# Expert weights in 16 KB runs laid out for them, four turned banks, a scatter in two groups, and another order of steps before and after the experts

## The chip, the cores and the metric

The kernel runs on one core of a Trainium2 chip. The core has TensorE (PE, matrix products into the 8 banks of PSUM), VectorE (DVE), ScalarE (ACT), GpSimd (POOL) and SyncE (SP), which issues most of the transfers from HBM to SBUF; 16 DMA engines carry them. The metric is the device time of one execution in microseconds (us), the median of the runs shown.

## The reference

Two layers follow each other on x of 512 tokens by 1024 channels, all float32.

```
def first_block(...):
    h = rmsnorm(x, norm1_g);  p = h @ w_in            # 1024 -> 1536
    c = centred_depthwise_conv(lru_x, conv_w, conv_b)
    h_f, h_b = rglru(c, ..., reverse=False), rglru(c, ..., reverse=True)
    y_lru = gelu(lru_gate) * (h_f + h_b);  y_four = fourier_mix(four_in)
    x = x + concat(y_lru, y_four) @ w_out
    x = x + expert_choice_moe(rmsnorm(x, norm2_g), w_router, w_gate, w_up, w_down)
    return rmsnorm(x, normf_g)

def expert_choice_moe(h, ...):                        # 16 experts, 64 tokens each
    gate, idx = top_k(softmax(h @ w_router).T, 64)    # each expert picks its tokens
    g, u = xin @ w_gate[e], xin @ w_up[e]             # xin = h[idx]; 1024 -> 2048
    eo = (silu(g) * u) @ w_down[e]                    # 2048 -> 1024
    out[idx] += gate * eo

def second_block(...):
    q, k, v, z_a, u, z_s, g_a, g_s = split(rms_norm(x, gain) @ w_in_2)
    y_a = (band_attention(q, k, v, rel_bias) * silu(z_a)) @ w_attn_out
    y_s = (glu(gelu(s5_ssm(u, ...))) * silu(z_s)) @ w_ssm_out
    return rms_norm(x + (sigmoid(g_a) * y_a + sigmoid(g_s) * y_s) @ w_out_2, final_gain)
```

The expert weights are 16 x 3 x 1024 x 2048 numbers, 402.65 MB, and each is read once.

## The kernel before, in words

The engines run what the source writes in the order in which it writes it; waits come from the data and from buffers that come free.

**Stage 1** (line numbers of the kernel before): `in_proj` units (weights in [128, 1024] pieces of 512 KB, loaded and split into a high and a low part by `Stream`, lines 126 to 159), convolution, gates, recurrence, Fourier part, `w_out`, router. A product of two float32 operands is three matmuls (`mm3`, lines 120 to 123): high by high, high by low, low by high. A "unit" is 24 such matmuls with 512 columns. The sums of squares of x go through ACT late (line 344), then the diagonal matrices `dg` (line 348) and one matmul (line 360) give `rr`, by which all projections are scaled.

**Experts.** Per expert e the 64 chosen tokens are gathered by matmuls (line 924), turned into `xT`, multiplied with gate and up (line 1062, 64 pairs of columns halves: gate into the upper, up into the lower 64 rows of the four PSUM tiles `gu0` to `gu3`), copied to SBUF (`copy`, lines 1042 and 1044), turned by PE (`turn`, line 1049) into the two `tp` banks, `silu` and `product` give the quarters of `hTe`, and the down product follows (line 1085) into `dn0` and `dn1`. The result of expert e - 1 is added into the tokens by `scatter` (line 960: four matmuls for each block of 128 tokens, four blocks) between the gate and up steps d = 2 to 5 of expert e.

The weights come in tiles of 1 MB, 8 KB for each of 128 partitions, through `prefetch` (line 172) into named places: 3 tiles of `ring`, 10 of `ringb` (only up to expert 5), 2 of `wr`, 3 of `wp`, and four that are used once (`sh`, `shw`, `h2n`). When PE has used a tile, `refill` issues the next one into its place: the order of the weights is fixed, and SP waits for each place in turn. 22 tiles lie ready when the first expert starts. The last expert's down weights come in pieces of 1 KB (line 185). Between these steps `side()` runs small pieces of the second layer's tables on DVE, ACT and PE.

**Stage 3**, after the experts: projections of the second layer, the chunked state space model (`chunk_inputs`, `chunk_scan`, `chunk_states`, `chunk_outputs`), `values(0)` to `values(3)` (24 matmuls each, the product for v), `turn_outputs` (the outputs to `Yc`, and on to DRAM), then the attention over 8 heads, in which each head's scores (lines 1371 and 1372), softmax and products are interleaved with `fill` units (24 projections in all: z_a, z_s, the two gates). `bt` is the table of relative biases, loaded by ACT's queue (line 1316), and corrected by POOL (lines 1317 and 1318); `att` holds the head's split q and k, of which POOL zeroes one part (line 1323). What is left of the 24 `fill` units runs after the heads (line 1420).

Of the kernel before, what the change touches and what calls it, by code (L numbers as in the profile page):

```python
# [54 lines left out]
NRING = 3  # L55
NRINGB = 10
# [4 lines left out]
def body(ctx, tc, a, out, dbg=None):  # L61
# [15 lines left out]
    wp = ctx.enter_context(tc.tile_pool(name="wp", bufs=3))  # L77
    wr = ctx.enter_context(tc.tile_pool(name="wr", bufs=2))
# [46 lines left out]
    class Stream:  # L125


        def __init__(self, units):
            self.units = list(units)
            self.loaded, self.done, self.n, self.half, self.held = [], [], 0, None, False  # L130

        def load(self, n=1):
            for _ in range(n):
                if self.units:
                    if self.half is None:
                        pair = wr.tile([128, 2, 1024], F32, name="w", tag="w")
                        t, self.half = pair[:, 0], pair[:, 1]
                    else:
                        t, self.half = self.half, None
                    SP.dma_start(t, self.units.pop(0))  # L140
                    self.loaded.append(t)

        def work(self, eng=None):
            if not self.loaded:
                return
            t = self.loaded.pop(0)
            s = wp.tile([128, 2, 1024], F32R, name="w", tag="w")
            s = Pair(s[:, 0], s[:, 1])
            s.put(slice(None), t, eng or (DVE if self.n % 3 == 2 else POOL))
            self.n += 1  # L150
            if not self.held:
                self.load()
            self.done.append(s)
# [7 lines left out]

    wq = []
    for e in range(NE):
        for k in range(DB):
            wq += [("g", e, k), ("u", e, k)]
        for k in range(8):
            wq.append(("d", e, k))
    wt, home = {}, {}
    wgu = {"g": a["w_gate"], "u": a["w_up"]}

    def prefetch(n=1, pool=None, skip=0, place=None):
        for _ in range(n):
            if not wq:
                return
            kind, e, k = key = wq.pop(skip)
            if place is None:
                home[key] = pool = pool or ring
                t = pool.tile([128, 2048], F32, name="w", tag="w")
            else:
                t = place  # L180
            if kind == "d" and e == NE - 1:

                v = t.rearrange("p (j b c) -> p j b c", j=2, b=4)
                for j in range(2):
                    SP.dma_start(v[:, j], bass.AP(tensor=a["w_down"].tensor, offset=a["w_down"].offset +
                                                  (e * FF + k % 2 * 1024 + j) * D + k // 2 * 256,
                                                  ap=[[2 * D, 128], [256 * D, 4], [1, 256]]))
            elif kind == "d":

                SP.dma_start(t, bass.AP(tensor=a["w_down"].tensor, offset=a["w_down"].offset + (e * FF + k * 256) * D,  # L190
                                        ap=[[2 * D, 128], [1, 2 * D]]))
            else:
                SP.dma_start(t, wgu[kind][e, k * 128:(k + 1) * 128, :])
            wt[key] = t

    def refill(e, *keys):

        for k in keys:
            p = home.pop(k, None)
            if p and (p is not ringb or e < EB):  # L200
                prefetch(1, p)
# [26 lines left out]
    with ExitStack() as c1:  # L228
# [5 lines left out]
        with ExitStack() as ca:  # L234
# [13 lines left out]
            for d in range(2, DB, 2):  # L248
                SP.dma_start(xT0[:, d:d + 2], a["xT"][:, d:d + 2])
            for tb in range(TB):  # L250
                SP.dma_start(xs[:, tb, :], a["x"][tb * 128:(tb + 1) * 128, :])
                if tb == 1:
                    ws.load()
            SP.dma_start(cst, a["cst"][:, 0:CCK])
            ws.load()
# [24 lines left out]
            for _ in range(12):  # L280
                PE.matmul(p[:, 0:128], ones, ones, start=True, stop=True)


            w = []
            for i in range(2):
                t = ws.loaded.pop(0)
                u = wp.tile([128, 2, 1024], F32R, name="w", tag="w")
                w.append((Pair(u[:, 0], u[:, 1]), t))
            ws.n = 2

            def half(i, j, eng):
                u, t = w[i]
                u.put((slice(None), slice(j * 512, j * 512 + 512)), t[:, j * 512:j * 512 + 512], eng)

            def part(d):
                hT.put((slice(None), d), xT0[:, d], DVE, scale=P("n1", d, d + 1))

            half(0, 0, DVE)
            part(0)
            part(1)  # L300
            half(1, 0, DVE)
            part(2)
            half(0, 1, POOL)
            part(3)
            half(1, 1, POOL)
            for d in range(4, DB):
                part(d)
            w = [u for u, t in w]

            two = [bank(), bank()]  # L310
            for k, i in [(k, i) for j in (range(2), range(2, 4), range(4, DB)) for i in range(2) for k in j]:
                mm3(two[i], w[i][:, k * 128:(k + 1) * 128], hT[:, k, :], start=(k == 0), stop=(k == DB - 1))
            ws.load(2)
            ws.work(DVE)
# [9 lines left out]
            act(ey, ey, AF.Exp, scale=-1.0)  # L324

# [8 lines left out]
            for q in (15, 13, 11, 9, 7, 5, 3, 1):  # L334
                DVE.tensor_mul(acc, acc, s2)
                DVE.tensor_scalar(acc, acc, 1.0 / q, None, op0=OP.add)
            DVE.tensor_mul(acc, acc, sv)
# [4 lines left out]
            act(rt, rt, AF.Sqrt)  # L342
            for tb in range(TB):
                act(early[:, 0:2].rearrange("p a b -> p (a b)"), xs[:, tb, :], AF.Square, accum_out=ss[:, tb:tb + 1])
            inv_sqrt(ta, ss, "n1", rt)
            dg = early2[:, 1]
            for tb in range(TB):
                DVE.tensor_scalar(dg[:, tb * 128:(tb + 1) * 128], ident, rt[:, tb:tb + 1], None, op0=OP.mult)
# [190 lines left out]
            for i, k in enumerate((5, 6, 7, 0, 1)):  # L539
                prefetch(NRINGB // 5, ringb, NRING + 7)  # L540
# [7 lines left out]
            prefetch(2, wr)  # L548
            prefetch(1, wp)
# [52 lines left out]
        shw = shared.tile([128, 2048], F32, name="shw", tag="Y")  # L602
        prefetch(2, wp)
        prefetch(NRING)
        prefetch(place=sh[:, 0:2048])
        prefetch(place=shw)
        for n in range(2):
            prefetch(place=h2n[:, 2 * n:2 * n + 2, :].rearrange("p t d -> p (t d)"))
# [274 lines left out]
    with c2:  # L883
# [7 lines left out]
        class Outputs:  # L891


            def __init__(self, e):
                t = shared.tile([128, 2, D], F32R, name="Y", tag="Y")
# [60 lines left out]
        def scatter(e, tb, halves=(0, 1)):  # L956
            for h in halves:
                p = tp()
# [54 lines left out]
        for e in range(NE):  # L1013
# [18 lines left out]

            hTe = sh[:, 0:1024].rearrange("p (k s) -> p k s", s=64)
            hTq = hTe.rearrange("p (j k) s -> p k j s", j=2)
            gus, tps = {}, {}

            def copy(n):
                gus[n] = t = sh[:, 1024 + n % 2 * 512:1536 + n % 2 * 512]
                o = t.rearrange("p (q j c) -> p q j c", q=2, j=2)
# [261 lines left out]
    for q in range(3):  # L1301
        chunk_outputs(q)
# [337 lines left out]
```

## Time and profile before

| | |
|---|---|
| median of 3 runs | 1538.53 us (1536.11 to 1540.04) |
| profiled execution | 1536.9 us, its span 1535.1 us |
| mean granted TensorE clock | 0.983 |
| PE busy | 1457.6 us (95%) |
| DVE, ACT, POOL busy | 607.4, 403.1, 184.0 us |
| DMA | 461.77 MB, 301 GB/s over the span |
| expert part | from 197 to some 1121 us of the span |

The span is the time from the first to the last instruction. PE is marked busy nearly everywhere, the DMA engines only in the expert part; whether one or the other sets the pace there is read from the waits and from the rate, not from these shares.

### The profile page before, as it was taken

The numbers are of one execution on the slowest core, as the hardware profiler recorded it, in microseconds if no ns is written. First come the engines' busy times: TensorE is split into PE (matmuls) and PEld (weight loads), VectorE is DVE, ScalarE is ACT, GpSimd is POOL, SyncE is SP. The second block draws the span as 40 slices with busy tenths as digits, with TensorE's granted clock in tenths as the row PEclk, the third lists the DMA queues.
The fourth block names the chain that finished last, engine by engine and source line by source line (L and its number), as shares of the span: only waits on it lengthen the run. The fifth ranks groups of instructions, "written<-read, shape, count | busy, mean of one in ns | idle before, by whom it ended". The sixth has DMA issues, their size and how long they took to land. (4 is left out here: it accounts for less than half of the span.)

```text
span 1535.1 us, 17258 instructions
## 1 busy us (share of the span) xinstructions
PE 1457.6 (95%) x6822; PEld 805.3 (52%) x6822; DVE 607.4 (40%) x1279; ACT 403.1 (26%) x690; POOL 184.0 (12%) x125
## 2 busy tenths in 40 slices
PE   7999899999999999999999999899999879999997
PEld 6778633333333334444334343343477757877886
DVE  6773512221222243333333332531354525554454
ACT  5654211100100121000100100210263146655533
POOL 2323000000001000000000001000022322113352
PEclk8999899999999999999999999999999989999999
DMA  7116989999999999999999999999927131222231
GB/s 276 55 55 264 371 331 407 426 428 426 427 427 417 426 426 426 427 427 426 427 426 427 427 428 406 413 421 427 382 87 137 56 101 65 83 83 94 99 124 55
DMA packets 88753, 461.77 MB, mean 301 GB/s; under 512 B 16670, under 2 KB 26270, under 8 KB 40416
## 3 DMA queue, kind: packets, MB, share of 16 engines
q1 hardware_dynamic: 86112, 456.14, 73.4%
q10 hardware_dynamic: 1904, 2.80, 0.6%
q0 software_dynamic: 656, 1.71, 0.4%
q8 instruction: 54, 0.88, 0.2%
q14 instruction: 27, 0.22, 0.0%
HBM read 455.25 MB, written 4.19 MB: 299 GB/s over the span
## 5 line engine op out<-in xcount | busy, mean ns | idle before, releaser
L1062 PE MATMUL gu<-w,xT 128*64 128x512 f32 x2032 | 471.8, 596 | 11.2 <-DMA w<-in_w_up_dram 9.9
L1062 PEld LDWEIGHTS gu<-w,xT 128*64 128x64 f32 x2032 | 167.5, 137 | 278.9 <-issue 229.5
L1085 PE MATMUL dn<-w,sh 128*64 128x512 f32 x944 | 217.4, 597 | 0.0
L962 DVE TENSOR_TENSOR xs<-tp,xs 128x512 f32<-128x512 f32 x120 | 77.5, 687 | 276.1 <-PE tp L960 276.1
L121 PE MATMUL ps<-hTh,w 128*128 128x512 f32 x384 | 156.1, 406 | 3.3 <-ACT hTh L110 1.8
L108 POOL TENSOR_TENSOR w<-w 128x1024 fp32r<-128x1024 f32 (+1 forms) x51 | 121.9, 2395 | 283.1 <-ACT w L107 247.8
L122 PE MATMUL ps<-hTl,w 128*128 128x512 f32 x384 | 153.8, 400 | 0.3 <-DVE hTl L111 0.3
L123 PE MATMUL ps<-hTh,w 128*128 128x512 f32 x384 | 153.2, 399 | 0.0
L1085 PEld LDWEIGHTS dn<-w,sh 128*64 128x64 f32 x944 | 63.7, 137 | 115.4 <-issue 115.0
L1042 ACT ACTIVATE sh<-gu 128x512 f32<-128x512 f32 x32 | 19.1, 597 | 396.5 <-PE gu L1062 394.7
L107 ACT ACTIVATE w<-w 128x1024 fp32r<-128x1024 f32 (+1 forms) x82 | 84.1, 1032 | 73.9 <-PE ps L123 43.5
L121 PEld LDWEIGHTS ps<-hTh,w 128*128 128x128 f32 x384 | 73.4, 191 | 22.5 <-issue 3.8
L122 PEld LDWEIGHTS ps<-hTl,w 128*128 128x128 f32 x384 | 73.7, 192 | 17.9 <-DVE hTl L111 0.6
L123 PEld LDWEIGHTS ps<-hTh,w 128*128 128x128 f32 x384 | 73.7, 192 | 17.6
L960 PE MATMUL tp<-Y,GT 128*128 128x512 f32 x240 | 72.3, 422 | 0.4 <-ACT ssm_BM L850 0.4
L108 DVE TENSOR_TENSOR w<-w 128x1024 fp32r<-128x1024 f32 (+1 forms) x31 | 39.5, 1277 | 73.4 <-ACT w L107 73.4
L960 PEld LDWEIGHTS tp<-Y,GT 128*128 128x128 f32 x240 | 40.1, 188 | 52.1 <-issue 44.6
L1044 DVE COPY sh<-gu 128x512 f32<-128x512 f32 x32 | 22.1, 691 | 105.6 <-PE gu L1062 71.5
L861 POOL DMA_DIRECT2D ssm_BM<-raw x8 | 4.2, 538 | 459.8 <-DVE raw L857 459.8
L929 ACT ACTIVATE xin<-tp 128x512 f32<-128x512 f32 x16 | 9.6, 597 | 188.7 <-PE tp L924 188.7
L935 DVE TENSOR_TENSOR xT<-tp,pp 128x512 f32<-128x512 f32 x16 | 11.1, 692 | 118.2 <-PE tp L933 118.2
L1049 PE MATMUL tp<-cst,sh 128*128 128x128 f32 x256 | 38.9, 285 | 17.0 <-DVE sh L1057 11.5
(441 smaller groups left out, 1769.9 us busy)
## 6 DMA issues: line engine op xcount, KB each, us to landing
w<-in_w_gate_dram SPq DMA_DIRECT2D x127, 1024.0 KB, 13.3
w<-in_w_up_dram SPq DMA_DIRECT2D x127, 1024.0 KB, 14.1
w<-in_w_down_dram SPq DMA_DIRECT2D x118, 1024.0 KB, 14.8
w<-in_w_dram SPq DMA_DIRECT2D x80, 512.0 KB, 4.3
w<-in_w_down_dram SPq DMA_DIRECT2D x16, 512.0 KB, 8.1
xs<-in_x_dram SPq DMA_DIRECT2D x4, 512.0 KB, 9.5
h2n<-in_w_down_dram SPq DMA_DIRECT2D x2, 1024.0 KB, 19.3
out_dram<-ga SPq DMA_DIRECT2D x8, 256.0 KB, 2.0
```

The lines of the kernel that those rows point to most:

```text
L107: act(h, src, AF.Copy)
L108: eng.tensor_tensor(l, src, h.bitcast(F32), op=OP.subtract)
L121: PE.matmul(p, x[0], y[0], start=start, stop=False)
L122: PE.matmul(p, x[0], y[1], start=False, stop=False)
L123: PE.matmul(p, x[1], y[0], start=False, stop=stop)
L960: PE.matmul(p, GT[e][:, tb * 128:(tb + 1) * 128], Yt[e][h * 512, 512][i], start=(i == 0), stop=(i == 1))
L962: DVE.tensor_add(sl, p, sl)
L1042: act(o, i, AF.Copy)
L1044: DVE.tensor_copy(o, i)
L1049: PE.transpose(p[:, j * 128:(j + 1) * 128], gus[n][:, j * 128:(j + 1) * 128], ident)
L1062: PE.matmul(gu[n][j * 64:j * 64 + 64], xt[:, d, :], wt[kind, e, d][:, n * 512:(n + 1) * 512], start=(d == 0), stop=(d == DB - 1))
L1085: PE.matmul(dn[n][j * 64:j * 64 + 64], hTe[:, k + 8 * j, :], w[:, j * 1024 + n * 512:j * 1024 + n * 512 + 512], start=(k == 0), stop=(k == 7))
```

## The change

1. **Weights laid out on the host.** Gate and up are joined: one tile holds, for each of 128 rows, 2048 gate and 2048 up numbers (16 KB). Four blocks of 128 rows of down make a tile of 16 KB too; for the last expert the tile holds a quarter of the columns of all 16 blocks, so that its 1 KB pieces are gone. A tile is 2 MB, 192 of them instead of 384.
2. **Places.** 2 tiles of `ring`, 5 of `ringb`, one over the four raw buffers of `Stream` (`raw4`), one in `spl2`, and two used once. The split parts of `Stream`'s units lie in `spl2` (two) and `spl1` (one); `Y` moves to `spl1`.
3. **Turned quarters.** The turned quarter n goes into the bank `gu{n}` that it was copied from; copies 2 and 3 have a buffer of their own, `gu2` (not in the last expert). The chunks of `hTe` are in natural order, so the down product begins with quarter 0.
4. **Scatter.** Blocks 0 and 1 after d = 3, blocks 2 and 3 after d = 5; odd blocks use the banks `dn0` and `dn1`.
5. **Stage 1.** x is loaded between the pieces of its transpose, its sums of squares are taken between the parts of `hT`, and `dg` is made before the last steps of the log-sigmoid series; 16 instead of 12 matmuls at the start; the third unit's split goes to POOL.
6. **Stage 3.** `values(1)` before `chunk_outputs(2)`; `bt` by POOL's queue, the zeroing of `att` ahead of the correction of `bt`; the first head's split before `values(3)`; two of the four copies of v on DVE; one `fill` unit before `turn_outputs`.

The core of the diff:

```
-NRING = 3
-NRINGB = 10
+NRING = 2
+NRINGB = 5
...
+    wsrc = {"g": a["wgu"], "d": a["wdn"]}
...
             kind, e, k = key = wq.pop(skip)
...
+            home[key] = pool = pool or ring
+            t = pool.tile([128, 4096], F32, name="w", tag="w")
+            t = t if isinstance(t, tuple) else (t,)
+            n = 4096 // len(t)
+            for i, o in enumerate(t):
+                SP.dma_start(o, wsrc[kind][e, k, :, i * n:i * n + n])
+            wt[key] = (lambda b, w, t=t, n=n: t[b // n][:, b % n:b % n + w])
...
+    def refill(e, key):
+        p = home.pop(key, None)
+        if p is places["raw"] and not wq:
+            return True
+        if p and p not in places["once"] and (p is not ringb or e < EB):
+            prefetch(1, p)
...
-        def scatter(e, tb, halves=(0, 1)):
-            for h in halves:
-                p = tp()
+        def scatter(e, tb):
+            for h in range(2):
+                p = pdn.tile([128, 512], F32, name=f"dn{h}") if tb % 2 else tp()
...
             def turn(n):
-                p = tp()
+                p = pgu.tile([128, 512], F32, name=f"gu{n}")
...
-                if e and 2 <= d < 2 + TB:
+                if e and d in (3, 5):
+                    scatter(e - 1, d - 3)
                     scatter(e - 1, d - 2)
...
-            for f, n in ((copy, 0), (copy, 1), (turn, 0), (turn, 1), (copy, 2), (silu, 0), (copy, 3), (product, 0),
-                         (silu, 1), (product, 1), (turn, 2), (turn, 3), (silu, 2), (product, 2), (silu, 3),
+            for f, n in ((copy, 0), (copy, 1), (turn, 0), (turn, 1), (copy, 2), (copy, 3), (turn, 2), (silu, 0),
+                         (product, 0), (turn, 3), (silu, 1), (product, 1), (silu, 2), (product, 2), (silu, 3),
                          (product, 3)):
...
-    for q in range(3):
+    for q in range(2):
         chunk_outputs(q)
     values(1)
+    chunk_outputs(2)
     values(2)
     Yc = stile("cos", [128, 32, 64], "Yc")
     chunk_outputs(3)
-    values(3)
-    for q in range(4):
-        turn_outputs(q)
...
-    ACT.dma_start(bt, bass.AP(tensor=a["rel"].tensor, offset=a["rel"].offset, ap=[[1, 128], [384, 8], [1, 256]]))
-    POOL.tensor_tensor(bt, bt, bfar[:, :, None].to_broadcast([128, 8, 256]), op=OP.subtract)
-    POOL.memset(bt[0:64, :, 0:64], -1e30)
+    POOL.dma_start(bt, bass.AP(tensor=a["rel"].tensor, offset=a["rel"].offset, ap=[[1, 128], [384, 8], [1, 256]]))
...
     split_head(0)
+    values(3)
...
+    fill()
+    for q in range(4):
+        turn_outputs(q)
+    for tau in range(8):
+        SP.dma_start(ys[:, tau, :].rearrange("(g c) n -> c g n", c=16), Yc[tau * 16:(tau + 1) * 16])
     for hp in range(4):
...
+    g["wgu"] = np.concatenate([x[n].reshape(NE, DB, 128, FF) for n in ("w_gate", "w_up")], 3)
+    w = x["w_down"].reshape(NE, 4, 4, 128, D).transpose(0, 1, 3, 2, 4).reshape(NE, 4, 128, 4096).copy()
+    w[NE - 1] = x["w_down"][NE - 1].reshape(16, 128, 4, 256).transpose(2, 1, 0, 3).reshape(4, 128, 4096)
```

The instructions at three places. On ACT, where the second expert goes over from gate and up to down (L1042 in the kernel before and L1049 in the changed one are copies of a quarter, L1053 and L1060 the silu), stands before:

```order
L1042 ACTIVATE sh<-gu_1675 128x512
L1053 ACTIVATE sh<-tp 128x2x2x64
L1042 ACTIVATE sh<-gu_1677 128x512
L1053 ACTIVATE sh<-tp 128x2x2x64 x3
L929 ACTIVATE xin<-tp 128x512
```

and in the changed kernel:

```order
L1049 ACTIVATE sh<-gu_1612 128x512
L1049 ACTIVATE gu_1615<-gu_1614 128x512
L1060 ACTIVATE sh<-gu_1729 128x256
L1060 ACTIVATE sh<-gu_1734 128x256
L1060 ACTIVATE sh<-gu_1741 128x256
L1060 ACTIVATE sh<-gu_1748 128x256
L938 ACTIVATE xin<-tp 128x512
```

The second copy has moved ahead of the first silu, and the silus read the four `gu` banks instead of the two `tp` banks.

On ACT in stage 3, from the outputs `y` of the state space model to the first head's softmax (`w` and `split` are the splits of weight units, `att` the head's split), stands before:

```order
L1269 ACTIVATE y<-ps 128x512 x3
L107 ACTIVATE w<-w 128x1024 x2
L1269 ACTIVATE y<-ps 128x512
L107 ACTIVATE w<-w 128x1024
L1276 ACTIVATE Yc<-ps 128x512 x4
L1311 ACTIVATE vt<-ps,stat 128x512 x4
L1316 DMA bt<-in_rel_dram 128x8x256
L1330 ACTIVATE att<-qk 64x512
L1331 ACTIVATE att<-qk 64x512
L1333 ACTIVATE att<-qk 64x512
L1381 ACT_TABLE_LOAD
```

and in the changed kernel:

```order
L1279 ACTIVATE y<-ps 128x512
L1334 ACTIVATE att<-qk 64x512
L1335 ACTIVATE att<-qk 64x512
L1337 ACTIVATE att<-qk 64x512
L109 ACTIVATE split<-raw_67 128x1024
L1347 ACTIVATE vt<-ps,stat 128x512 x2
L109 ACTIVATE split<-raw_67 128x1024
L1368 ACT_TABLE_LOAD
L1368 ACTIVATE za<-fl 128x512
L1286 ACTIVATE Yc<-ps 128x512 x4
L1399 ACT_TABLE_LOAD
```

The head's split has moved from behind the eight copies of `Yc` and `vt` to the place right after the last `y`, a `fill` unit's silu (`za`) stands in between, and the load of `bt` has left ACT.

On POOL at the same place stands before:

```order
L1253 TENSOR_TENSOR gq<-gq,ssm_cos 128x512 x2
L108 TENSOR_TENSOR w<-w 128x1024 x2
L1317 TENSOR_TENSOR bt<-bt,bfar 128x2048
L1318 MEMSET bt 64x8x64
L1323 MEMSET att 64x512 x2
```

and in the changed kernel:

```order
L1263 TENSOR_TENSOR gq<-gq,ssm_cos 128x512 x2
L110 TENSOR_TENSOR split<-raw_67,split 128x1024 x2
L1320 DMA bt<-in_rel_dram 128x8x256
L1325 MEMSET att 64x512 x2
L1326 TENSOR_TENSOR bt<-bt,bfar 128x2048
L1327 MEMSET bt 64x8x64
```

The zeroing of `att` stands ahead of the correction of `bt`, and POOL issues the load of `bt` itself.

## Rows read from the trace of the kernel before

**Rows 1.** PE's waits, whole span: who waited for whom, us, times, longest.

```profile
PE tp L1049 <- DVE sh L1057: 11.5, 20, 0.7
PE gu L1062 <- DMA w<-in_w_up_dram: 9.9, 8, 2.2
PE ps L360 <- DVE early L348: 4.9, 1, 4.9
PE ps L1371 <- ACT att L1333: 4.9, 1, 4.9
```

**Rows 2.** Stretches: length, busy us by engine, granted clock, DMA share, GB/s.

```profile
6.00:14.00 8.00, 6.19 (x19) 4.74 (x20) 6.10 (x7) 7.10 (x12) 3.04 (x2) 0.79 1.02 419
280.00:480.00 200.00, 196.69 (x914) 71.29 (x912) 47.38 (x89) 17.79 (x35) 0.00 (x0) 1.00 1.01 427
1092.00:1106.00 14.00, 11.20 (x79) 7.39 (x80) 5.28 (x10) 3.99 (x8) 0.20 (x1) 0.88 1.07 375
640.00:1040.00 400.00, 384.05 (x1734) 160.30 (x1732) 144.57 (x368) 41.28 (x79) 5.14 (x9) 1.00 1.01 423
```

**Rows 3.** DVE in order of time, the xT of experts 7 and 15.

```profile
572.46 0.69 DVE L935 TENSOR_TENSOR xT<-tp,pp 128x512 f32<-128x512 f32 x1 [5.57 <-PE tp L933]
...
1050.58 0.69 DVE L935 TENSOR_TENSOR xT<-tp,pp 128x512 f32<-128x512 f32 x1 [9.42 <-PE tp L933]
```

**Rows 4.** PE in order of time in experts 8 and 15.

```profile
645.96 1.19 PE L960 MATMUL tp<-Y,GT 128*128 128x512 f32 x4
...
672.26 1.46 PE L1049 MATMUL tp<-cst,sh 128*128 128x128 f32 x8 [0.68 <-DVE sh L1057]
...
1062.84 3.65 PE L1062 MATMUL gu<-w,xT 128*64 128x512 f32 x14 [1.00 <-DMA w<-in_w_up_dram]
```

**Rows 5.** PE in stage 3, in order of time; two stretches as in rows 2.

```profile
1213.54 0.48 PE L1267 MATMUL ps<-ssm_W,Hs 128*64 128x128 f32 x1 [4.86 <-DVE Hs L1254]
...
1216.82 0.50 PE L121 MATMUL ps<-w,hTh 128*128 128x512 f32 x1
...
1222.50 0.40 PE L121 MATMUL ps<-w,hTh 128*128 128x512 f32 x1
...
1228.18 0.45 PE L1266 MATMUL ps<-ssm_BM,U 128*64 128x128 f32 x4
...
1230.13 0.50 PE L121 MATMUL ps<-w,hTh 128*128 128x512 f32 x1
...
1235.81 1.91 PE L1275 MATMUL ps<-cst,y 128*128 128x128 f32 x16
...
1249.44 0.58 PE L1372 MATMUL ps<-att 128*128 128x256 f32 x1 [6.28 <-POOL att L1323]
...
1251.74 0.63 PE L121 MATMUL ps<-hTh,w 128*128 128x512 f32 x1
...
1213.50:1216.80 3.30, 3.26 (x30) 3.10 (x30) 2.50 (x3) 0.60 (x1) 0.61 (x1) 0.56 0.03 5
1249.40:1254.00 4.60, 4.56 (x13) 3.89 (x14) 3.74 (x12) 3.19 (x8) 0.52 (x1) 0.50 0.00 0
```

**Rows 6.** POOL in stage 3; two transfers: queue, KB, us to landing.

```profile
1244.63 3.60 POOL L1317 TENSOR_TENSOR bt<-bt,bfar 128x2048 f32<-128x2048 f32 x1 [18.28 <-DMA bt<-in_rel_dram]
...
bt<-in_rel_dram ACTq DMA_DIRECT2D x1, 1024.0 KB, 6.7
...
bfar<-in_rel_dram POOLq DMA_DIRECT2D x1, 4.0 KB, 6.1
```

**Rows 7.** DVE and POOL in stage 1, in order of time.

```profile
26.28 5.11 DVE L348 TENSOR_SCALAR early<-cst,rt 128x128 f32<-128x128 f32 x4
...
26.27 4.64 POOL L108 TENSOR_TENSOR w<-w 128x1024 fp32r<-128x1024 f32 x2 [12.52 <-DVE rt L221]
```

**Rows 8.** PE and DVE after the last head, in order of time.

```profile
1406.38 2.37 PE L1405 MATMUL ps<-big,vt 128*64 128x512 f32 x16
...
1410.04 2.49 DVE L108 TENSOR_TENSOR yapl<-qk,yaph 128x512 fp32r<-128x512 f32 x4
```

More of the change, by code (lines that the diff above doesn't have):

```diff
@@ L129, in __init__, with place @@
             self.units = list(units)
-            self.loaded, self.done, self.n, self.half, self.held = [], [], 0, None, False
+            self.loaded, self.done, self.m, self.n, self.due, self.held = [], [], 0, 0, 0, False
+            self.two = self.one = None
         def load(self, n=1):
[L133 to L141, printed above, removed]
+            self.due += n
+            while self.due and self.units and len(self.loaded) < 4:
+                t = raw4[:, self.m % 4]
+                self.m += 1
+                self.due -= 1
+                SP.dma_start(t, self.units.pop(0))
+                self.loaded.append(t)
+        def place(self):
+            i = self.n % 3
+            self.n += 1
+            if i == 2:
+                self.one = s = self.one or spl1.tile([128, 2, 1024], F32R, name="split", tag="w")
+            else:
+                self.two = self.two or spl2.tile([128, 2, 2, 1024], F32R, name="split", tag="w")
+                s = self.two[:, i]
+            return Pair(s[:, 0], s[:, 1])
         def work(self, eng=None):
@@ L146, in work @@
             t = self.loaded.pop(0)
[L147 to L150, printed above, removed]
+            eng = eng or (DVE if self.n % 3 == 2 else POOL)
+            s = self.place()
+            s.put(slice(None), t, eng)
             if not self.held:
@@ L279, in body @@
             p = bank()
-            for _ in range(12):
+            for _ in range(16):
                 PE.matmul(p[:, 0:128], ones, ones, start=True, stop=True)
[L284 to L314, printed above, removed]
             ls = ta.tile([128, 8], F32, name="ls")
@@ L336, in body @@
                 DVE.tensor_scalar(acc, acc, 1.0 / q, None, op0=OP.add)
+            inv_sqrt(ta, ss, "n1", rt)
+            dg = early2[:, 1]
+            for tb in range(TB):
+                DVE.tensor_scalar(dg[:, tb * 128:(tb + 1) * 128], ident, rt[:, tb:tb + 1], None, op0=OP.mult)
             DVE.tensor_mul(acc, acc, sv)
@@ L601, in body @@
         sh = shared.tile([128, 2048], F32, name="sh")
-        shw = shared.tile([128, 2048], F32, name="shw", tag="Y")
-        prefetch(2, wp)
+        places["once"] = [Fixed(sh[:, 0:2048], lambda: spl1.tile([128, 2048], F32, name="w", tag="w")), Fixed(h2n.rearrange("p t d -> p (t d)"))]
+        prefetch(1, spl2)
         prefetch(NRING)
[L605 to L608, printed above, removed]
+        for p in places["once"]:
+            prefetch(1, p)
         tk = c1.enter_context(tc.tile_pool(name="tk", bufs=1, side="right"))
```

172 lines of the change are left out of this document (92 added, 80 removed).

## The prediction

> **What bounds the kernel now.** I read the waits of PE first. They are short almost everywhere [rows 1, 5]: no single wait exceeds 6.3 us, and in the expert part the most that one group adds up to is 11.5 us (the second turn, waiting for DVE's product) and 9.9 us (gate and up, waiting for weights). That looks like a PE-bound kernel. The second view contradicts it: in the stretches of the expert part the 16 DMA engines are busy all the time, a share of 1.01 at 423 to 427 GB/s [rows 2]. Between 640 and 1040 us PE is busy 384.05 of 400 us, so it has 16 us to spare there, 2.4 us for each of the 6.7 experts, while DMA has nothing. The third view gives the pace: from the xT of expert 7 to that of expert 15 it is 478.12 us, 59.77 for each expert [rows 3], and the 25.17 MB of one expert at 427 GB/s take 58.9 us. So from about expert 7 on the transfers set the pace, and PE's small waits for weights are what shows of it. That lasts to the last wait for weights, at 1062.84 us, in the third step of the last expert's gate and up [rows 4]; behind it PE has all its weights and sets the pace itself, to the end of the kernel, except where another engine is late. There are three such places in stage 3, of 4.86 us (`Hs` from DVE), 4.9 us (the first head's split on ACT) and 6.28 us (the zeroed half of `att` on POOL) [rows 1, 5], and one in stage 1, of 4.9 us for `dg` [rows 1].
>
> **Weights in 16 KB runs.** Each run is served by one DMA engine. At a share of 1 an engine takes 16 times the run's length over the rate: with 1 KB runs (375 GB/s) 43.7 ns, with 8 KB (427) 307 ns [rows 2]. The 4 KB runs of stage 1 (419 GB/s) give 156.4 ns and lie on the same straight line: 263.3 ns for 7168 more bytes, which is 27.2 GB/s for an engine, and 5.8 ns that a run costs whatever its length. A run of 16 KB would then take 608 ns, and 16 engines move 431.1 GB/s, 1.0% more. (The 1 KB stretch holds other transfers too, so the 5.8 ns are known to about a third.) The bytes that must flow until the last waited-for tile: 402.65 MB, less the 22 tiles that lie ready (23.07 MB; the new places hold as much), less what is loaded behind that wait (five pairs of gate and up, 10.49 MB, and the down part, 8.39 MB), is 360.7 MB. At 427 GB/s that takes 844.7 us, at 431.1 it takes 836.7: **-8.0 us**. The lower end is no gain, if the fixed cost isn't one of a run but of a smaller piece; the upper end is 435 GB/s, the slope alone, 829.2 us, or -15.5. I take the line's value, since three stretches lie on it. PE can follow: it needs 0.56 us less for each expert and has 2.4 to spare.
>
> The Trainium skill ("DMA: Bandwidth & Descriptors", section "Why small descriptors are slow") has a fixed cost of about three cycles for a packet, with 32 bytes in a cycle: 8 KB would be 256 of 259 cycles and 16 KB 512 of 515, a gain of 0.6%, by estimate 5 us in place of 8. The rows' slope gives a larger fixed cost than that; the sum keeps the rows' value.
>
> **Larger tiles.** A place comes free once for 2 MB, after gate and up of a step, no longer in two halves. While the first expert runs and all places are full, DMA idles until the first is free; that is up to one step of PE later (8 matmuls, 2.1 us, by the 3.65 us of 14 [rows 4]), half of it in the mean. I take **+1 us**, from 0 to +4.
>
> **Turned quarters and scatter.** Own banks take the second turn's wait for DVE's product away (11.5 us in 20 times, 0.68 for one [rows 1, 4]) and the scatter in two groups spares changes of work between gate and up (the four matmuls take 1.19 us [rows 4]; their order and number are unchanged). In experts 7 to 14 this lies behind the transfers and counts nothing; in experts 1 to 6 PE runs ahead into the same full queue, so it also only moves the wait. What counts is the last expert, whose last turns and scatters lie behind 1062.84 us: one wait of 0.68 and some tenths at the changes, **-1.5 us**, from 0 to -2.5. If transfers stopped being the bound, all of it would count, about 1 us an expert. The price is the copy into `gu2`, in buffers that `xin` used, and a scatter's odd blocks in `dn0` and `dn1`, which are idle until the down product; nothing is late there.
>
> **Stage 1.** `dg` is made of 4 pieces (5.11 us, while POOL splits a unit beside them in 4.64 us [rows 7]), and PE waits 4.9 us for it [rows 1]. The squares now come between the parts of `hT` on ACT, and `dg` before the last steps of the series, perhaps 3 us earlier in DVE's order; against that, the third unit's split moves from DVE to POOL, and POOL still works beside DVE, so its matmuls start later. I take **-1 us**, from +3 (the split later by its own length) to -5 (the wait gone).
>
> **Stage 3.** Three waits go, and I follow what is late next at each.
> - `values(1)` takes 1216.82 to 1222.50, 5.68 us, and now lies where PE waited for `Hs` from 1208.68 to 1213.54 [rows 5]. It covers the 4.86 us with 0.8 to spare. Its weights must be split by 1208.7, as they were ahead of 1216.8; those splits were done early on POOL and ACT, which the new split places keep in order.
> - The first head's split on ACT came behind eight copies, and cost 4.9 us [rows 1]. It now follows the last `y`, and `values(3)` (5.68 us from 1230.13, [rows 5]) and one `fill` cover it.
> - POOL waited 18.28 us for `bt`, which ACT's queue issued late, corrected it for 3.60 us and only then zeroed `att` [rows 6], for which PE waited 6.28 [rows 5]. Now the zeroing stands first. `bt` is issued by POOL's queue behind the last weight splits; behind it on POOL stand the zeroing, the correction and then the splits of the next `fill` units. The transfer took 6.7 us on ACT's queue, and POOL's 4 KB one 6.1 us with the same number of pieces per partition [rows 6]; I take 7 to 9. With the buffer free at about 1223, `bt` is there at 1232, corrected at 1236, and PE comes to the scores at about 1237: tight, but the scores' addition of `bt` is DVE's and a `fill` unit lies between.
>
> The waits are 4.86 + 4.9 + 6.28 = 16.0 us. Beyond them, PE ran at the lower clock after each idle stretch: granted 0.56 and 0.50, the 1.2 GHz level, for 3.3 and 4.6 us after the two waits [rows 5]. `chunk_outputs(2)` took 3.28 us (1213.54 to 1216.82), `chunk_outputs(3)`, at full clock, 1.95 (1228.18 to 1230.13): 1.33 us lost. At half clock the 4.6 us behind the second wait are 2.3 at full, of which I count 2.1: 3.4 in all. One thing is given back: one `fill` is spent early, so the last one no longer stands between the last head and the output product. PE ends the head at 1408.75 (1406.38 + 2.37), and the first `yapl` that it needs comes at 1410.04 + 0.62 [rows 8], a new wait of **+2.0 us**. Sum: -16.0 - 3.4 + 2.0 = **-17.4 us**, with bounds of -10 (`bt` late) and -20 (no new wait).
>
> **The sum.** -8.0 + 1.0 - 1.5 - 1.0 - 17.4 = -26.9 us. The profiled execution took 1536.9 us (its span 1535.1), the median of the runs is 1.6 above it; -26.9 makes 1510.0 of the profile and 1511.6 of the median. I say **1511 us**.
>
> **The rivals.**
> - *Run length gains nothing* (the engines cut a run into pieces of 8 KB or less, or cost goes by bytes). For it: 4 to 8 KB gave only 2%, in different stages. The change is then 1 - 1.5 - 1 - 17.4 = -18.9: 1519.6 by the median. Chance 0.18.
> - *Stage 3 keeps a wait.* `bt`'s 1024 pieces are slow to issue on POOL's queue, the correction is late, and the splits of the next `fill` weights, queued behind it on POOL, hold PE. If half of 16.0 + 3.4 stays, the time is 1521. Chance 0.11.
> - *The rate reaches the slope's 435 GB/s*: 7.5 us better, 1504. Chance 0.07.
> - *Slower: 16 KB rows side by side cost rate.* The 128 rows of a tile now lie 16 KB apart in place of 8. If the engines' streams then meet in the memory, the rate falls, and each percent costs 8.5 us of the 844.7. All other gains (18.9) are gone when it falls by 2.2%, below 417.6 GB/s. The lowest rate at a full share is 375 GB/s [rows 2]; the 360.7 MB would take 961.9 us, +117, and the kernel 1637. Against it: nothing in the trace ties a rate to a pitch; 4 KB and 8 KB pitches run at nearly the same rate. Chance 0.04.
>
> The Trainium skill speaks for this last one in the same page's section "Latency and other measured facts": copies with a row pitch of 512 KiB ran at 207 GB/s, of 2 MiB at 164, as streams collide. Its pitches are far above 16 KB, and no run here shows such a one.
>
> **How the numbers follow.** The forecast has 0.60. Its own range is 1506 to 1517, from the bounds of stage 1, of the larger tiles and of `bt`. Both milder rivals lie at 1520 to 1521, the better one at 1504; so 1502 to 1524 leaves out the slow one and the far ends of the others, no more than 2 in 10. What a measurement of this kernel can tell from no change is about 0.3%, 4.6 us; all cases but the slower one lie 17 us or more below 1538.5: faster 0.94, same 0.02 (the rate falls by about the deciding 2.2%), slower 0.04.
>
> **What would show it.** Right: a stretch of the middle experts at 430 to 432 GB/s with the DMA share still 1.0, and 59.2 us from expert to expert; no wait of PE over 1.5 us between the end of the experts and the heads, the granted clock 1.00 throughout there; a new wait of about 2 us of the output product for `yapl`. Wrong: a rate of 427 or less (first rival, or the last); PE waiting for weights at a DMA share below 1, which would make the larger tiles the bound; POOL's correction of `bt` ending after PE reaches the first scores, or PE waiting for a split queued behind it; in stage 1 a wait for `dg` as long as before, or a new one for the third unit's split.

## The result, and the profile after

The changed kernel takes 1512.66 us in the median (1511.45 to 1514.0, 4 runs) against 1537.32 us of the kernel before on the same chip; the ratio is 0.9841, with a 95% interval of 0.9818 to 0.9863. The prediction said 1511 us, 1502 to 1524. The profiled execution has a span of 1512.2 us, 22.9 us less than before; the prediction's sum was 26.9.

Where it went is read by four places that both kernels pass: the xT of experts 0, 6 and 15, and the first product of stage 3. Each row is a time since the start of the span.

PE and DVE of the changed kernel at these places, in order of time:

```profile
197.75 0.69 DVE L944 TENSOR_TENSOR xT<-tp,pp 128x512 f32<-128x512 f32 x1 [5.80 <-PE tp L942]
...
509.19 0.69 DVE L944 TENSOR_TENSOR xT<-tp,pp 128x512 f32<-128x512 f32 x1 [9.98 <-PE tp L942]
...
1046.67 0.69 DVE L944 TENSOR_TENSOR xT<-tp,pp 128x512 f32<-128x512 f32 x1 [9.49 <-PE tp L942]
...
1116.84 0.50 PE L123 MATMUL gu<-hTh,split 128*128 128x512 f32 x1 [0.80 <-ACT split L109]
```

The kernel before at the same places (expert 15 stands in [rows 3]):

```profile
196.62 0.69 DVE L935 TENSOR_TENSOR xT<-tp,pp 128x512 f32<-128x512 f32 x1 [5.49 <-PE tp L933]
...
516.11 0.69 DVE L935 TENSOR_TENSOR xT<-tp,pp 128x512 f32<-128x512 f32 x1 [9.42 <-PE tp L933]
...
1121.38 0.50 PE L121 MATMUL gu<-hTh,w 128*128 128x512 f32 x1 [0.79 <-ACT w L107]
```

| part | before, us | after, us | difference |
|---|---|---|---|
| to the xT of expert 0 | 196.62 | 197.75 | +1.1 |
| expert 0 to expert 6 | 319.49 | 311.44 | -8.0 |
| expert 6 to expert 15 | 534.47 | 537.48 | +3.0 |
| expert 15 to stage 3 | 70.80 | 70.17 | -0.6 |
| stage 3 to the end | 413.72 | 395.36 | -18.4 |

So stage 3 gave most of it, and the experts 5.0 us up to the last one. The first and the fourth row are too small to be read from one trace each: in the eleven traces on record whose stage 1 is the changed kernel's, the xT of expert 0 comes between 195.3 and 200.0 us, on both sides of the 196.62 before, and in the traces of the changed kernel's variants the fourth part takes 68.3 to 72.2 us. Stage 3 repeats well: in eight of nine traces with the changed stage 3 it takes 395.4 to 395.6 us, in the ninth, that of the 4 KB runs, 397.1. PE's waits in the changed kernel, whole span (total, times, longest):

```profile
PE gu L1069 <- DMA w<-in_wgu_dram: 38.2, 40, 2.0
PE gu L1056 <- DVE sh L1051: 4.1, 3, 2.1
...
PE ps L372 <- DVE early L355: 2.6, 1, 2.6
```

Against [rows 1], the three waits of stage 3 are gone and so is the turn's 11.5 us; in its place PE waits four times as long for weights (38.2 us, before 9.9). That is what a PE that got faster under a bound that hardly moved looks like. The rates, by stretches as in [rows 2], of the changed kernel:

```profile
280.00:480.00 200.00, 200.00 (x948) 75.61 (x948) 47.66 (x90) 17.81 (x35) 2.33 (x1) 1.00 1.01 430
560.00:760.00 200.00, 187.07 (x884) 69.67 (x882) 71.60 (x201) 20.77 (x37) 0.00 (x0) 1.00 1.01 429
```

and of the kernel before:

```profile
560.00:760.00 200.00, 192.64 (x880) 81.96 (x876) 73.41 (x204) 21.00 (x37) 0.00 (x0) 1.00 1.01 426
```

The DMA share is 1.01 in both, and the rate rose from 427 to 430 and from 426 to 429 GB/s, 0.7%. From expert 7 to expert 15 an expert takes 59.52 us (570.49 to 1046.67 for eight), before 59.77; the prediction had named 59.2 as a sign of being right.

### The profile page after: what moved, and what is told of

The parts are those of the page before. It is cut to its first block, busy times and chain, and to the rows that moved or that the text cites. A ratio compares the mean times of both kernels' runs of the same rounds, so it can differ in the third digit from the quotient of the medians.

```text
span 1512.2 us, 16864 instructions
## 1 busy us (share of the span) xinstructions
PE 1431.0 (95%) x6830; PEld 777.2 (51%) x6830; DVE 609.3 (40%) x1280; ACT 402.4 (27%) x689; POOL 188.6 (12%) x127
## 4 chain that ended last, share of the span: by engine, by line
PE 68%; DMA 20%; DVE 6%; issue 2%; ACT 2%; POOL 1%; ACTq 0%; POOLq 0%; DVEq 0%
PE gu L1069 17%; DMA w<-in_wgu_dram 17%; PE dn L1095 13%; PE ps L123 7%; PE ps L124 7%; PE ps L125 7%; PE tp L933 4%; DMA w<-in_wdn_dram 3%; PE gu L1056 1%; DVE cT L402 1%; PE dn L1118 1%; PE tp L969 1%; PE dn L969 1%; PE tp L942 1%; PE ps L1423 1%
## 5 line engine op out<-in xcount | busy, mean ns | idle before, releaser
L1069 PE MATMUL gu<-w,xT 128*64 128x512 f32 x1656 | 375.2, 598 | 39.1 <-DMA w<-in_wgu_dram 38.2
L1069 PEld LDWEIGHTS gu<-w,xT 128*64 128x64 f32 x1656 | 114.0, 137 | 282.8 <-issue 204.5
L110 POOL TENSOR_TENSOR split<-raw,split 128x1024 fp32r<-128x1024 f32 (+1 forms) x52 | 125.3, 2415 | 274.9 <-ACT split L109 263.1
L123 PE MATMUL ps<-hTh,split 128*128 128x512 f32 x384 | 155.2, 404 | 2.6 <-DVE early L499 1.5
L124 PE MATMUL ps<-hTl,split 128*128 128x512 f32 x384 | 153.0, 398 | 1.9 <-DVE hTl L113 1.9
L125 PE MATMUL ps<-hTh,split 128*128 128x512 f32 x384 | 152.6, 398 | 0.8 <-POOL split L110 0.8
L1049 ACT ACTIVATE sh<-gu 128x512 f32<-128x512 f32 x17 | 10.2, 597 | 416.5 <-PE gu L1069 411.1
L109 ACT ACTIVATE split<-raw 128x1024 fp32r<-128x1024 f32 (+1 forms) x82 | 84.0, 1031 | 64.6 <-PE ps L125 31.4
L1069 PE MATMUL gu<-raw,xT 128*64 128x512 f32 x384 | 87.2, 596 | 0.2
L123 PEld LDWEIGHTS ps<-hTh,split 128*128 128x128 f32 x384 | 73.0, 190 | 22.6 <-issue 3.6
L124 PEld LDWEIGHTS ps<-hTl,split 128*128 128x128 f32 x384 | 72.9, 190 | 20.5 <-DVE hTl L113 3.6
L125 PEld LDWEIGHTS ps<-hTh,split 128*128 128x128 f32 x384 | 72.9, 190 | 18.3 <-POOL split L110 1.3
L110 DVE TENSOR_TENSOR split<-raw,split 128x1024 fp32r<-128x1024 f32 (+1 forms) x30 | 38.2, 1277 | 62.4 <-ACT split L109 62.4
L933 PE MATMUL tp<-h2n,G 128*64 128x512 f32 x224 | 52.9, 593 | 1.5 <-DVE G L927 1.5
```

The costliest lines, as they stand in the source:

```text
L109: act(h, src, AF.Copy)
L110: eng.tensor_tensor(l, src, h.bitcast(F32), op=OP.subtract)
L123: PE.matmul(p, x[0], y[0], start=start, stop=False)
L124: PE.matmul(p, x[0], y[1], start=False, stop=False)
L125: PE.matmul(p, x[1], y[0], start=False, stop=stop)
L933: PE.matmul(p[h * 64:h * 64 + 64], G[:, tb, :], src[:, tb, h * 512:(h + 1) * 512], start=(tb == 0), stop=(tb == TB - 1))
```

## The experiments

Ratios are to the kernel before, on the same chip, and are compared with the changed kernel's 0.9841.

**8 KB runs.** Each tile in twice as many transfers:

```
-                SP.dma_start(o, wsrc[kind][e, k, :, i * n:i * n + n])
+                for j in range(0, n, 2048):
+                    SP.dma_start(o[:, j:j + 2048], wsrc[kind][e, k, :, i * n + j:i * n + j + 2048])
```

> The changed kernel with each 2 MB tile fetched by twice as many transfers, in runs of 8 KB (the rows stay 16 KB apart). If the length of a run sets the rate (429.5 GB/s in the middle experts of the changed kernel, 426.4 in the kernel before), the rate falls back to about 426.4 and 845 us of transfers grow by 0.7%, 6 us: about 1518.5 us. If the larger tiles, their places or the distance of the rows give the rate, it stays at 429 to 430 GB/s and the time at 1512 to 1513 us.

1522.7 us, ratio 0.9909 (0.9892 to 0.9927). The same two stretches:

```profile
280.00:480.00 200.00, 199.70 (x935) 75.07 (x935) 47.08 (x89) 16.43 (x32) 2.47 (x1) 1.00 1.01 426
560.00:760.00 200.00, 190.33 (x874) 74.84 (x872) 72.54 (x204) 20.92 (x37) 0.00 (x0) 1.00 1.01 423
```

The rate fell, as the first theory says, and in the second stretch, where the transfers set the pace, further than expected, to 423 GB/s. The time grew by 10 us in place of 6. From expert 0 to 15 the trace takes 856.41 us (196.26 to 1052.67) against 848.92.

**4 KB runs.** The same with steps of 1024 numbers.

> The same in runs of 4 KB. If a run costs a fixed time beside its bytes, the two rates (8 and 16 KB) give 4.3 ns a run, and 4 KB runs flow at 420.6 GB/s: 18 us more than the changed kernel, about 1530 us. By the 5.8 ns of the prediction it is 419 GB/s and 1533 us. If the engines cut every run into pieces of 4 KB or less, nothing changes: 1512 to 1513 us.

1539.51 us, ratio 1.0013 (1.0002 to 1.0023): the whole gain is gone, 26.9 us, and more than either forecast of 1530 and 1533 us, since the rate fell below the 419 to 420.6 GB/s that they took.

```profile
280.00:480.00 200.00, 196.38 (x918) 73.67 (x916) 46.63 (x88) 16.03 (x31) 0.00 (x0) 1.00 1.03 417
560.00:760.00 200.00, 187.45 (x850) 71.44 (x851) 70.73 (x197) 21.28 (x41) 0.00 (x0) 1.00 1.03 414
```

So the engines don't cut every run into pieces of 4 KB or less. From the first stretch of the three kernels (430, 426, 417 GB/s) a run takes 609.6, 307.7 and 157.2 ns of an engine: twice the 8 KB run less the 16 KB run is 5.8 ns, twice the 4 KB run less the 8 KB run 6.7 ns. The second stretch (429, 423, 414 GB/s) gives 8.7 and 6.7 ns in the same way, and the kernel before's 8 KB runs (427 and 426) against the 16 KB runs give 4.3 in both. So a run costs 4 to 9 ns beside its bytes, and the 5.8 ns of the prediction lie in the middle.

**8 KB runs, packed.** As the first, with each half tile in one piece in HBM:

```
+                    SP.dma_start(o[:, j:j + 2048], wsrc[kind][e, k, (i * n + j) // 2048])
...
+    for n in ("wgu", "wdn"):
+        g[n] = np.ascontiguousarray(g[n].reshape(NE, -1, 128, 2, 2048).transpose(0, 1, 3, 2, 4))
```

> As the run with 8 KB runs, but each half tile lies in one piece in HBM, so that the rows of a transfer are 8 KB apart, not 16. There the rate was 423.5 GB/s, below the 426.4 of the kernel before. If the distance of the rows costs that, the rate goes back to 426.4 and the time falls by 0.7% of 845 us, from 1522.7 to about 1517 us. If the distance doesn't matter and twice as many transfers for a place do it, it stays at 423.5 GB/s and 1522 to 1523 us.

1522.44 us, ratio 0.9889 (0.987 to 0.9907), and the second stretch stands at 423 again:

```profile
560.00:760.00 200.00, 190.10 (x876) 74.41 (x876) 73.11 (x204) 20.92 (x37) 0.00 (x0) 1.00 1.01 423
```

So 8 or 16 KB between the rows makes no difference to 8 KB runs. Why 8 KB runs reach 423 GB/s here and 426 in the kernel before was not settled; two transfers into one place instead of one into each of two is one thing that differs still.

**Half of the bytes.** The second half of each tile of experts 6 to 14 is left out, and the matmuls read the first half twice, so that PE's work stays:

```
...
+                m = n // 2 if 6 <= e < NE - 1 else n
+                SP.dma_start(o[:, 0:m], wsrc[kind][e, k, :, i * n:i * n + m])
+            wt[key] = (lambda b, w, t=t, n=n, m=m: t[b // n][:, b % n % m:b % n % m + w])
```

> The changed kernel with only half of each tile of experts 6 to 14 transferred; the matmuls read the loaded half twice (the up products read gate's weights, the down products half of down's), so all of PE's work stays and half of the bytes go. If the transfers set the pace, it falls from 59.5 us an expert to PE's own, 52.6 to 55 us, and the kernel ends 35 to 55 us earlier, at 1458 to 1478 us. If PE sets the pace, 1508 to 1513 us.

1465.96 us in one run, 46.7 us less. PE is busy 287.55 of 290 us, and the transfers have room:

```profile
640.00:930.00 290.00, 287.55 (x1386) 113.44 (x1384) 108.00 (x295) 27.46 (x52) 4.22 (x8) 1.00 0.68 232
```

An expert takes 54.7 us (509.84 to 1002.24 for nine) in place of 59.7. So the transfers do set the pace from expert 6 on.

**Old turns and scatter.** `turn` into `tp()` with `sh` as its source, the old order of `copy`, `silu` and `product`, and `scatter` in four steps:

```
-                p = pgu.tile([128, 512], F32, name=f"gu{n}")
+                p = tp()
...
-                if e and d in (3, 5):
-                    scatter(e - 1, d - 3)
+                if e and 2 <= d < 2 + TB:
                     scatter(e - 1, d - 2)
```

> The changed kernel with the turned quarters in the two tp banks and the scatter in four steps, as before. PE runs expert 2 to 5 in 52.57 us each in the changed kernel and in 54.5 in the kernel before, so these parts are worth 1.95 us an expert where PE sets the pace. If the transfers set the end of the experts, only the last expert's tail counts, +1.5 us: about 1514 us. If PE sets it, all 15 count, +29 us: about 1541 us.

1520.84 us, ratio 0.99 (0.9885 to 0.9914): 8 us, neither 1.5 nor 29. Both theories fell. The trace shows where: expert 0 to 6 takes 319.71 us (199.95 to 519.66), as in the kernel before, and towards its end the transfers run dry. Two stretches of this kernel:

```profile
480.00:500.00 20.00, 20.00 (x89) 7.26 (x90) 5.49 (x9) 0.36 (x1) 4.38 (x2) 1.00 0.90 365
500.00:520.00 20.00, 19.17 (x96) 7.29 (x94) 5.28 (x13) 2.86 (x7) 0.00 (x0) 1.00 1.00 413
```

and of the changed kernel:

```profile
480.00:500.00 20.00, 18.41 (x92) 7.87 (x90) 8.21 (x17) 2.65 (x6) 2.05 (x2) 1.00 1.01 428
```

The kernel before has the same turns and a PE as late, but tiles of 1 MB, and dips much less:

```profile
480.00:500.00 20.00, 19.32 (x90) 7.63 (x88) 5.85 (x10) 1.85 (x4) 4.43 (x2) 1.00 0.99 406
```

In both kernels with tiles of 2 MB the five places of `ringb` are not filled again from here on. Few places are left, each is free only when PE has used its 2 MB, and a PE that is 8.3 us late there holds the transfers up, share 0.90. Afterwards they set the pace, so what they lost there stays lost: by expert 15 the two kernels are 5.3 us apart (854.22 against 848.92 us from expert 0). Of the 8.5 us between the two spans another 0.8 lie behind expert 15, and 2.2 ahead of expert 0, where the edit changes nothing. This gave a new theory, that only the speed of PE ahead of expert 7 counts, and two runs for it. No run changed the number of places alone, so that their number makes the dip is argued from its time, not shown.

**Old turns and scatter from expert 7 on.** `turn`, `copy` and `scatter` as in the run before where e >= 7, as changed where e < 7.

> The changed kernel with turned quarters and scatter as before from expert 7 on, and as changed ahead of it. Undone everywhere they cost 8.2 us, and the trace of that run has lost 8.3 us by the start of expert 6 (311.4 to 319.7 us from expert 0's start), with the transfers idle in part around 490 us. If only PE's pace ahead of expert 7 counts, where it makes places free, and the rest hides behind the transfers, this run loses the last expert's tail alone: about 1514 us. If each expert counts alike, half of the loss: about 1517 us or more.

1513.46 us, ratio 0.9834 (0.9818 to 0.9851): not distinguishable from the changed kernel. The stretch from 480 us shows no gap:

```profile
480.00:500.00 20.00, 18.21 (x92) 7.89 (x92) 8.21 (x17) 2.65 (x6) 1.15 (x2) 1.00 1.01 427
```

So nine of the sixteen experts can have the old turns for nothing that can be measured, and the loss is that of the experts ahead of them.

**Old scatter alone.** Four steps through `tp`, new turns.

> The changed kernel with the scatter in four steps through tp, as before, and the turned quarters in their new banks. Both parts undone cost 8.2 us. If PE's time for an expert up to expert 5 is what counts, this costs the scatter's share of it: the turns' share is the second turn's wait and the copies behind it, some 1.3 of the 1.95 us an expert, so the scatter's is 0.6, and the time some 1515 us. If the scatter's order makes no difference to PE, 1512 to 1513 us; if all of it was the scatter, 1520 us.

1511.87 us, ratio 0.9822 (0.9808 to 0.9837): the scatter in two groups is worth nothing that can be measured, although it makes an early expert longer, 53.3 us against 52.57 (experts 2 to 5: 295.29 to 455.19 for three). A loss of 0.73 us an expert leaves the transfers fed (427 GB/s at a share of 1.01 from 480 to 500 us), one of 2.0 doesn't.

**values(1) back.**

```
-    for q in range(2):
+    for q in range(3):
         chunk_outputs(q)
     values(1)
-    chunk_outputs(2)
```

> The changed kernel with values(1) behind chunk_outputs(2), as before. If PE's idle time in front of chunk_outputs(2) was Hs being late and nothing else, the wait of some 4.9 us comes back, and with it the lower clock behind it (1.3 us): +6 us, about 1519 us. If Hs now comes earlier, or the other new covers absorb the wait, the time stays at 1512 to 1514 us.

1520.29 us, ratio 0.9891 (0.9873 to 0.991), 7.6 us. PE and one stretch of this kernel:

```profile
1208.04 0.47 PE L1277 MATMUL ps<-ssm_W,Hs 128*64 128x128 f32 x1 [4.89 <-DVE Hs L1264]
...
1209.00:1212.50 3.50, 3.50 (x26) 3.07 (x23) 2.01 (x4) 0.68 (x2) 1.26 (x1) 0.50 0.45 151
```

The wait is back as it was (4.86 in [rows 5]), with a granted clock of 0.50, the 1.2 GHz level, behind it. Stage 3 takes 402.80 us (1115.90 to 1518.7) against 395.36: 7.4, so 2.5 us beside the wait, twice the prediction's 1.33. The low clock lasts longer here than in the kernel before: 0.50 up to 1212.5 us and 0.87 in the next 3.5 us, against 0.56 for 3.3 us.

**The head's split back.** `split_head(0)` behind the copies of v, all of them on ACT, `bt` by ACT's queue behind these, its correction ahead of the zeroing, no early `fill`:

```
-    POOL.dma_start(bt, bass.AP(tensor=a["rel"].tensor, offset=a["rel"].offset, ap=[[1, 128], [384, 8], [1, 256]]))
...
+    ACT.dma_start(bt, bass.AP(tensor=a["rel"].tensor, offset=a["rel"].offset, ap=[[1, 128], [384, 8], [1, 256]]))
+    POOL.tensor_tensor(bt, bt, bfar[:, :, None].to_broadcast([128, 8, 256]), op=OP.subtract)
+    POOL.memset(bt[0:64, :, 0:64], -1e30)
...
-    fill()
```

> The changed kernel with the first head's split behind the copies of v, bt loaded by ACT's queue behind it, corrected ahead of the zeroing of att, all copies of v on ACT and no early fill. If the two waits of 4.9 and 6.3 us and the clock behind them (2.1 us) are the head's, they come back, and the 1.5 us at the last head go: +11.8 us, about 1524.5 us. If the gain of stage 3 came from values(1) alone, 1512 to 1514 us.

1525.1 us, ratio 0.9917 (0.9901 to 0.9934), 12.4 us. Two waits of this kernel, which answer to 4.86 and 6.28 before:

```profile
1232.51 0.58 PE L1384 MATMUL ps<-att 128*128 128x256 f32 x1 [4.85 <-ACT att L1327]
...
1239.33 0.58 PE L1385 MATMUL ps<-att 128*128 128x256 f32 x1 [6.24 <-POOL att L1345]
```

Stage 3 takes 406.70 us (1117.60 to 1524.3), 11.3 more. With the 7.4 of values(1) that is 18.8, and the change gained 18.4: the two parts are all of it.

**No early fill.**

```
-    fill()
     for q in range(4):
         turn_outputs(q)
```

> The changed kernel without the fill unit ahead of turn_outputs, so that one is left behind the last head. If that unit only moved the bubble, PE has no wait at the first scores (they need no bt, and two fill units follow), and the 1.5 us between the last head and the output product go: about 1511.2 us. If the unit covers the correction of bt and the weight split queued behind it on POOL, a wait of 2 to 4 us stands after the first scores: 1513 to 1516 us.

1511.47 us, ratio 0.983 (0.9813 to 0.9846); the interval overlaps that of the changed kernel. The trace decides: between 1195 and 1420 us PE has no wait left, and stage 3 takes 393.45 us (1117.35 to 1510.8), 1.9 less. The early unit covers nothing and makes the bubble at the last head.

**Late splits on DVE.** The two weight splits behind `dg`:

```
-            ws.work(POOL)
+            ws.work(DVE)
+            ws.work(DVE)
```

> The changed kernel with the two weight splits behind dg on DVE instead of POOL. If POOL's splits hold up the four pieces of dg (5.17 us together beside POOL), they take some 1.3 us alone, PE's 2.57 us wait for dg goes and the matmul for rr begins at about 30.7 instead of 33.2 us: 2 us less in all, about 1510.7 us. If the pieces take 1.3 us each by themselves, dg stays at 5.2 us, the splits come later, and it is 1512 to 1515 us.

1510.59 us, ratio 0.9829 (0.9812 to 0.9847), which alone doesn't separate it either. The four pieces of `dg` on DVE in this kernel:

```profile
28.31 0.88 DVE L355 TENSOR_SCALAR early<-cst,rt 128x128 f32<-128x128 f32 x4
```

0.88 us in place of 5.17. PE's wait for them is gone, and the matmul for `rr` begins at 30.81 us instead of 33.20:

```profile
30.81 1.02 PE L373 MATMUL ps<-early 128*128 128x512 f32 x2
```

**Both of these.** Late splits on DVE and no early fill:

> The changed kernel with the two weight splits behind dg on DVE and without the early fill unit. The two took 2.1 and 1.2 us off by their medians, at different places of the path that sets the end (before the experts, and after the heads). If both lie on it, they add up: about 1509.4 us. If the earlier start of the experts is lost to the transfers, it is the early fill's alone: about 1511.5 us.

1507.9 us, ratio 0.9797 (0.9783 to 0.9812), faster than both kernels: 0.4% below the changed one, and the intervals don't meet. Both parts stand in its trace: `rr` begins at 30.98 us, and stage 3 takes 393.41 us (1114.69 to 1508.1). The 4.8 us by the medians are more than the 3.3 of the two runs together; the runs of one kernel lie up to 4 us apart, so it stays open whether the parts add up exactly.

## Why the prediction came out right, and where its steps did not

**The bound** was read rightly. Between 640 and 1040 us a DMA share of 1.01 said more than a PE that is busy for 96%: with half of the bytes an expert falls from 59.7 to 54.7 us.

**16 KB runs**: the mechanism held, and the size was 8.0 us for what the rate makes 5.9. The prediction said 431.1 GB/s at 16 KB; 430 stands where it had read 427, a rise of 0.7% and not 1.0%, and 0.7% of 844.7 us is 5.9. Its 5.8 ns follow from its 4 KB and 8 KB stretches; the slope that stands beside them, from 1 KB to 8 KB, goes with 6.1. Going back to 8 KB runs costs 7.5 us between experts 0 and 15 and 10 us in the medians, but those runs flow slower than the 8 KB runs of the kernel before. The Trainium skill's three cycles a packet ("DMA: Bandwidth & Descriptors", section "Why small descriptors are slow") give, by estimate, 0.6% from 8 to 16 KB and 1.2% from 4 to 8. The rows have 0.7 to 1.4% (426 to 429, 423 to 429) and 2.2% (417 to 426), so the measured cost is the larger one, by little against the kernel before, and the measurement decides.

**Turned quarters and scatter** is the step that failed. "In experts 1 to 6 PE runs ahead into the same full queue, so it also only moves the wait" was true of the scatter and false of the turns. Where the number of places falls, at expert 5 and 6, the queue is no longer full, and a late PE starves the transfers (with the old turns 365 GB/s at a share of 0.90 from 480 to 500 us). The 1.5 us taken for the last expert's tail are not seen: it took 0.6 us less than before, but with the old turns 71.0 and 68.3 us in two runs, on both sides of the 70.2. Undoing turns and scatter cost 8 us by the medians, and in the traces 8.3 us up to expert 6, of which 5.3 are left at expert 15.

**Larger tiles**: the +1 us came out, but only with the turns beside it. If the experts gained by the rate alone, the 853.96 us between experts 0 and 15 would become 848.0 (by 427 to 430, and the same by 426 to 429; the rates are read to 1 GB/s, which is some 2 us of it). The changed kernel takes 848.92, 0.9 more. With the old turns it takes 854.22, 6.2 more, and the change of the weights gains nothing at all. So the larger tiles cost some 6 us with a PE as late as before, the new turns take 5.3 of these away, and the prediction, which priced the two apart, has neither. It looked for the cost in the first expert, and there it is not: in the 85 us from the xT of expert 0 the rate is 392 of 430 GB/s in the changed kernel and 388 of 427 before, 91% in both. No run had 1 MB tiles in the new places, so this is worked out and not shown.

**Stage 1** did not gain its 1.0 us, by the cause that the prediction had named for its upper bound. At the xT of expert 0 the traces lie too far apart to tell a sign, but the matmul for `rr` begins later in every trace with this stage 1, at 32.8 to 33.5 us. Before and after:

```profile
31.44 2.07 PE L360 MATMUL ps<-early 128*128 128x512 f32 x2 [4.86 <-DVE early L348]
```

```profile
33.20 1.89 PE L372 MATMUL ps<-early 128*128 128x512 f32 x2 [2.57 <-DVE early L355]
```

PE's wait for `dg` is half as long, because PE gets there later, with new waits ahead of it, one of them for the third unit's split:

```profile
PE ps L124 <- DVE hTl L113: 1.9, 5, 0.7
...
PE ps L125 <- POOL split L110: 0.8, 1, 0.8
```

The 16 matmuls at the start, for which the prediction had no term, leave PE 0.32 us of waiting ahead of the first product where it waited 1.82, and from 8 to 12 us the granted clock is 1.00, in all thirteen traces with this start, and was 0.57 before; no run took them out alone. The third unit's split went to POOL, and DVE stood still beside it. DVE and POOL of the changed kernel:

```profile
22.92 2.27 DVE L350 TENSOR_TENSOR acc<-acc,s 128x8 f32<-128x8 f32 x1
25.43 0.17 DVE L350 TENSOR_TENSOR acc<-acc,s 128x8 f32<-128x8 f32 x1
...
27.98 5.17 DVE L355 TENSOR_SCALAR early<-cst,rt 128x128 f32<-128x128 f32 x4
```

```profile
22.80 2.38 POOL L110 TENSOR_TENSOR split<-raw,split 128x1024 fp32r<-128x1024 f32 x1 [7.62 <-ACT split L109]
27.96 4.71 POOL L110 TENSOR_TENSOR split<-raw,split 128x1024 fp32r<-128x1024 f32 x2 [2.79 <-DVE rt L229]
```

An instruction of 0.17 us takes 2.27 while POOL's split runs, and ends when it ends. So `dg` begins 1.7 us later than before (27.98, [rows 7] 26.28) and takes as long as before. The Trainium skill ("Trainium Architecture — The Big Picture", section "What this means for kernel authors") calls the port pair of these two engines an exclusive lock; by it DVE loses the whole of POOL's time. These rows agree: DVE loses 2.10 of the 2.26 us that POOL's split still runs, and 4.29 of the 4.71.

**Stage 3** was right in its places and nearly in its size, -18.4 for -17.4. The three waits are gone, the granted clock is 1.00 from 1200 to 1390 us, and `bt` came in time, as POOL of the changed kernel shows (before: [rows 6]):

```profile
1225.90 3.60 POOL L1326 TENSOR_TENSOR bt<-bt,bfar 128x2048 f32<-128x2048 f32 x1 [4.20 <-DMA bt<-in_rel_dram]
```

It is corrected at 1229.50, and PE comes to the first scores at 1232.21. The new bubble was 1.5 us for 2.0. With the waits' 16.0 us gone and the bubble added, the 18.4 leave 3.9 us for the clock behind the waits, for the 3.4 taken.

PE after the last head, in the changed kernel:

```profile
1387.27 2.38 PE L1423 MATMUL ps<-big,vt 128*64 128x512 f32 x16
1390.86 0.50 PE L123 MATMUL ps<-yaph,split 128*128 128x512 f32 x1 [1.21 <-ACT yaph L109]
1391.67 0.50 PE L124 MATMUL ps<-yapl,split 128*128 128x512 f32 x1 [0.31 <-DVE yapl L110]
```

**The rivals.** Of the rival that run length gains nothing, and of slower 16 KB rows, nothing is left: the run itself gives the rate, and rows 8 or 16 KB apart flow alike. The slope's 435 GB/s were not reached, and ahead of the last head stage 3 has no wait over 0.8 us left. The colliding streams that the prediction quotes from the Trainium skill for far larger pitches are given there as an inference, not as verified, and no run here tests them. That the time fell in the middle of the range is in part luck: the cost of the larger tiles and the worth of the turns, some 5 us each and both left out, are the same microseconds seen from two sides.

## What to carry to other kernels

Where transfers set the pace with a share of 1, a compute engine's saving can still be worth most of its size (here 5.3 of 8.3 us) if it comes ahead of the moment when fewer and larger buffers are left, because the transfers can starve there; look for the stretch in which the share dips below 1, and ask how late the engine is just there. A stall of PE can cost more than its length (a wait of 4.89 us cost 7.4), since the granted clock is low behind it; price the stretch behind the wait too. Look at what POOL runs beside a chain of small DVE instructions before moving work to POOL.

## What the runs showed of the hardware

A run of 4, 8 or 16 KB cost an engine 4 to 9 ns beside its bytes, depending on which two rates are compared. The runs changed the number of transfers with the length of a run, so it isn't shown which of the two carries that time. Four DVE instructions on 128x128 took 0.88 us alone and 5.17 us beside two POOL instructions of 4.71 us together.
